# Opening a kernel from a list of steps, with fourteen of its transposes turned ahead of the first product

## The chip, the cores and the metric

The kernel runs on one core of a Trainium2 chip. The metric is device time in microseconds of one execution, the median over several runs. The engines that matter are TensorE (matmuls and transposes; the profile's PE, with PEld for the loading of its stationary operand), VectorE (DVE), ScalarE (ACT), GpSimd (POOL) and SyncE (SP), which here only issues DMAs. Each engine works through its own instructions in order; between engines, instructions wait on semaphores.

## The reference, cut to what matters

One layer of a diffusion backbone: 128 context tokens and 1024 latent tokens with 1024 features are normalized and modulated, projected by one weight matrix into two groups of attention heads (queries, keys, values, gates), run through a global and a windowed attention, gated, projected back and added to the residual stream.

```python
shift, scale, gate = modulation(c, w_mod[l], b_mod[l])          # silu(c) @ w_mod + b_mod
h = rmsnorm(xs, norm_gain[l]) * (1.0 + scale) + shift
q_a, k_a, v_a, g_a, q_b, k_b, v_b, g_b = project(h, w_in[l], ...)
...
xs = xs + gate * merge_out(o_a, g_a, o_b, g_b, w_out[l])
```

The change concerns only how `h` is made, and the first product with it: the gates `g_a` of group A.

## The kernel before, in words

Tokens are cut into nine tiles of 128 (`x` tile 0 is the context, 1 to 8 are latent), features into eight blocks of 128, numbered j or k. The products need `h` with features on the partitions, so each 128x128 block of `x` is transposed on TensorE against an identity (`turned`, line 606) into a PSUM bank, and from there `transposed` (line 610) makes `h`: ScalarE applies scale and shift of block j (line 617, into `hf`), VectorE casts the result to the high part of `h` (line 622), and GpSimd subtracts that from `hf` to get the low part (line 623). Every product is made of three matmuls: high weight by high `h`, low by high (lines 467, 468) and high by low (line 463). Tokens stand in the order 1, 2, ..., 8, 0 and are cut into three groups of 512, 256 and 384 columns (`THIRDS`): tiles 1 to 4, tiles 5 and 6, tiles 7, 8 and 0.

Ahead of a transpose an x tile is normalized: `norm` (line 589) squares it on ScalarE with a running sum (line 594; for tile 4 the second half on VectorE, line 597), GpSimd turns the sum into a reciprocal root (lines 601 and 603), and `scaled` multiplies the tile by it in place (line 587 on VectorE, 585 on ScalarE). Scale and shift of block j come from `modulate_rows(j)` (line 545: 16 small matmuls of the modulation weights `wm[j]`, 1 MB each, and a copy `mrows` out of PSUM, line 556) and `modulate(j)` (line 558: two transposes of `mrows`, then `columns`, lines 568 to 572, which fill `a_mod` and `b_col`). The weights of the gates arrive as eight chunks `rawga` of 256 KB (three buffers); `high` casts a chunk on ScalarE (line 435), `low` makes the rest on VectorE (line 440) and issues the load of a further chunk (line 443).

The opening is the part from the start to the end of the gate product of the first two token groups. Its order is written out by hand as a loop over j = 0 to 9 (line 661) with tables beside it (`LOADS`, `WARM`, `TURNED`, `BEHIND`, `PAIRED`). The first passes do this: tiles 1 and 2 are normalized and scaled on VectorE, 16 matmuls on the identity keep TensorE busy (`warm`, line 628), `modulate_rows(0)`, the two transposes of block 0 of tiles 1 and 2, `modulate(0)`, norms of tiles 3 and 4, then `h` of block 0 and its product in halves (`first_half`, line 642, its matmuls on line 648). From j = 2 each pass makes `modulate_rows(j)`, then the product of block j - 1 for four output blocks (`first_gates`, line 639) into four PSUM banks `big`, and between its parts `modulate`, the weights' split and `transposed(j, 1, 4, 0)`, that is four transposes for tiles 1 to 4. Later passes add the transposes of tiles 5 to 8 and 0, and the product of the second group (`next_gates`, line 651) into two banks `small`. At the end the product of the third group follows (`gates`, line 505). The transposes take two banks in turn, D and E (`bank_tr`); the eight banks are thus all named, but the four of `big` hold nothing until the first gate product.

All loads go through SP's queue in program order. A buffer is loaded again once its last reader is done: `wm` has three buffers, so wm3 follows `modulate_rows(0)`.

Of the kernel before, what the change touches and what calls it, by code (L numbers as in the profile page):

```python
# [11 lines left out]
F32 = mybir.dt.float32  # L12
# [8 lines left out]
P = 128  # L21
# [29 lines left out]
X_FROM = 2  # L51
SECOND_FROM = 5
LOADS = (1, 2, "m", 3, 4, "w", "m", "w", "m", 5, 6)
WARM = (16, 1, 5)
FULL = 1
MROWS_ACT = (7,)
SOON = 8
PAIRED = (4, 6)

TURNED = ((), (), (), (0,), (1, 2), (3,), (4, 5), (6, 7), (), ())  # L60
BEHIND = ((), (), (), (), (0,), (1, 2), (3,), (4, 5), (6,), (7,))
WIDE = 5
# [237 lines left out]
def hybrid_step(ctx, tc, x_prompt, x_sample, cache_k_a, cache_v_a, cache_k_b, cache_v_b,  # L300
# [48 lines left out]
    def bank_tr(name):  # L349
        turn["tr"] += 1  # L350
        return bank("DE"[turn["tr"] % 2], name)
# [53 lines left out]
    class Weights:  # L405
# [32 lines left out]
        def low(self, k, h, l):  # L438
            eng = nc.gpsimd if self.tag in POOL_LO and k % 2 else nc.vector
            eng.tensor_tensor(l, self.raw[k], h, op=ALU.subtract)  # L440
            self.hi.append(h)
            self.lo.append(l)
            self.load()
# [73 lines left out]
    with tc.tile_pool(name="st", bufs=2, side="right") as st:  # L517
# [9 lines left out]

        def load_wm(j):
# [45 lines left out]
        xn = {}  # L574

        def load_x(t):
            xn[t] = st.tile([P, D], F32, name=f"xn{t}", bufs=1)
            nc.sync.dma_start(xn[t], x_tile[t])
# [27 lines left out]
        def turned(px, j, t0, n):  # L606
            for i in range(n):
                nc.tensor.transpose(px[:, P * i : P * i + P], xn[t0 + i][:, P * j : P * j + P], ident)

        def transposed(j, t0, n, cond, px=None):  # L610
            if px is None:
                px = bank_tr(f"px{j}_{t0}")
                turned(px, j, t0, n)
# [3 lines left out]
            nc.scalar.activation(hf[:, :w], px[:, :w], AF.Identity,  # L617
                                 scale=a_mod[:, j, cond : cond + 1], bias=b_col[:, j, cond : cond + 1])
# [5 lines left out]

        for step in LOADS:
            load_x(step) if step in FIRST else W_GA.load() if step == "w" else load_wm(len(wm))

        def warm(n):

            for _ in range(n):  # L630
                nc.tensor.matmul(small[0], ident_b, ident_b.unsqueeze(1).to_broadcast([P, 4, P]), start=True, stop=True)

        rest = [7, 8, 0]
        second = [(j, 7, 2, 0) for j in range(WIDE)] + [(j, 0, 1, 1) for j in range(KT)]

# [19 lines left out]
        def more():  # L655
            ready = [x for x in second if x[0] <= j]
            if ready and j >= SECOND_FROM:
                second.remove(ready[0])
                transposed(*ready[0])

        for j in range(KT + 2):
            if j == 0:
                for t in (1, 2):
                    norm(t)
                    scaled(t)
                warm(WARM[0])
                modulate_rows(0)
                turned(small[1], 0, 1, 2)
                warm(WARM[1])
                modulate(0)  # L670
                warm(WARM[2])
                norm(3)
                norm(4, True)
                scaled(3, slice(0, 2 * P))
                transposed(0, 1, 2, 0, small[1])
                hi = W_GA.high()
                scaled(4, slice(0, 2 * P), nc.scalar)
                W_GA.low(*hi)
                first_half(0, 0)
                transposed(0, 3, 2, 0)  # L680
                modulate_rows(1)
                first_half(0, 1, 2)
                load_wm(3)
                continue
            if j == 1:
                modulate(1)
                W_GA.split()
                transposed(1, 1, 4, 0)
                first_half(1, 0, 1, 2)
                scaled(3, slice(2 * P, D))  # L690
                scaled(4, slice(2 * P, D), nc.scalar)
                load_wm(4)
                norm(5)
                continue
            big_on, behind = j <= KT, BEHIND[j]
            if SOON <= j < KT:
                W_GA.split()
            if j < KT:
                if j in PAIRED:
                    modulate_rows(j, j + 1)  # L700
                elif j - 1 not in PAIRED:
                    modulate_rows(j)
                if j + 3 < KT:
                    load_wm(j + 3)
                if X_FROM <= j < X_FROM + 3:
                    load_x(rest[j - X_FROM])
            if big_on:
                first_gates(0, j - 1, 0)
                first_gates(1, j - 1, 0)
            if j == 3:  # L710
                scaled(6)
            if 2 <= j < SOON:
                if j - 1 not in PAIRED:
                    modulate(*((j, j + 1) if j in PAIRED else (j,)))
                W_GA.split()
                transposed(j, 1, 4, 0)
            if big_on:
                first_gates(0, j - 1, 1)
                first_gates(1, j - 1, 1)
            if j == 2:  # L720
                norm(6)
                scaled(5)
            if big_on:
                first_gates(2, j - 1)
            if SOON <= j < KT:
                modulate(j)
                transposed(j, 1, 4, 0)
            if big_on:
                first_gates(3, j - 1)
            if X_FROM + 1 < j <= X_FROM + 4:  # L730
                scaled(rest[j - X_FROM - 2])
            for n in TURNED[j]:
                transposed(n, 5, 2 if n < WIDE else 4, 0)
            if X_FROM < j <= X_FROM + 3:
                norm(rest[j - X_FROM - 1])
            for ch in range(4):
                for n in behind:
                    next_gates(ch, n)
                if ch % 2 or j >= KT:
                    more()  # L740
            if j == KT:
                sg_tile.append(lambda n: st.tile([P, 512], F32, tag="sg", name=n, bufs=3))
                for ch in range(FULL):
                    put_gates(big[ch], 0, ch, slice(0, 512), nc.sync)
            if KT - 2 <= j < KT:
                raw = st.tile([P, KT, 2, P], F32, tag="wm", name=f"raw_qa{j}", bufs=3).rearrange(
                    "p (k a) s n -> p k (a s n)", a=2)
                k0 = 4 * (j - KT + 2)
                c0, n = W_QA.cols[0]
                nc.sync.dma_start(  # L750
                    raw, w_in[P * k0 : P * k0 + 512, c0 : c0 + n].rearrange("(k p) n -> p k n", p=P))
                W_QA.raw += [raw[:, k] for k in range(4)]
        assert not second


# [884 lines left out]
```

## Time and profile before

| what | us |
|---|---|
| median of 3 runs (668.84 to 669.23) | 669.11 |
| the profiled execution | 669.37 |
| its span, first to last instruction | 667.5 |
| TensorE busy in it | 655.5 |
| first gate product starts at | 14.78 |
| `modulate_rows(3)` starts at | 25.49 |
| product of the third group starts at | 66.9 |

Times within the profile count from the start of the span. A row of the timeline gives start, length, engine, line, operation, the output and input tiles, how often, and in brackets how long the engine stood idle before it and what released it. TensorE's matmuls overlap, and their ends are modelled, so the length of a single one is longer than the step from one to the next; the chain of waits gives the steps. Rows of groups give busy time, mean length in ns and idle time before them.

### The profile page before, as it was taken

How to read it: one execution, taken by the hardware profiler on the slowest of the kernel's cores; microseconds unless marked ns; L12 is line 12 of the kernel's file. 1: busy time of each engine (PE TensorE's matmuls, PEld its weight loads, DVE VectorE, ACT ScalarE, POOL GpSimd, SP SyncE). 2: the span in 40 equal slices, each digit the busy share in tenths (PEclk: the TensorE clock that was granted, in tenths of full speed). 3: DMA queues.
4: the chain of work that ended last, by engine and by line, in shares of the span. 5: the costliest groups of instructions: out<-in, count | busy, mean ns of one | idle time of the engine just before them, and what ended most of it. 6: DMA issues, size and time to landing. Idle time of an engine off the chain costs nothing.

```text
span 667.5 us, 10648 instructions
## 1 busy us (share of the span) xinstructions
PE 655.5 (98%) x3757; PEld 517.5 (78%) x3757; DVE 438.6 (66%) x924; ACT 281.3 (42%) x586; POOL 332.3 (50%) x324
## 2 busy tenths in 40 slices
PE   6999999999999999999999999999999999999997
PEld 2789988887788788997777777777777777777766
DVE  3566147786684766446768878688787786875533
ACT  4555411242142453435554355444454355434531
POOL 2457013332321232357885575657665675557712
PEclk9999999999999999999999999999999999999999
DMA  8980365437645211744142302223132212332233
GB/s 323 413 304 6 131 231 151 91 77 224 185 108 146 91 48 37 224 127 148 56 132 100 99 31 97 89 72 96 41 119 88 72 53 83 124 92 78 76 103 111
DMA packets 55837, 81.41 MB, mean 122 GB/s; under 512 B 7388, under 2 KB 26932, under 8 KB 54760
## 3 DMA queue, kind: packets, MB, share of 16 engines
q1 hardware_dynamic: 47752, 69.06, 30.9%
q10 hardware_dynamic: 8032, 11.68, 6.9%
q8 instruction: 30, 0.49, 0.3%
q14 instruction: 23, 0.19, 0.1%
HBM read 61.42 MB, written 19.29 MB: 121 GB/s over the span
## 4 chain that ended last, share of the span: by engine, by line
PE 92%; DVE 2%; ACT 2%; DMA 2%; issue 1%; ACTq 1%; SPq 0%; POOL 0%; DVEq 0%
PE pv L1432 15%; PE po L1507 15%; PE st L1390 7%; PE st L1391 7%; PE pmx L1130 5%; PE pq L454 4%; PE pq L455 4%; PE pq L453 4%; PE pg L468 3%; PE pg L463 3%; PE pg L467 3%; PE pk L454 2%; PE pk L455 2%; PE pk L453 2%; PE pmx L1133 2%; DMA xn<-in_x_sample_dram 1%
## 5 line engine op out<-in xcount | busy, mean ns | idle before, releaser
L1415 POOL TENSOR_TENSOR acc<-acc,pe 128x512 f32<-128x512 f32 x112 | 150.0, 1339 | 6.8 <-ACT pe L1402 0.6
L1402 ACT ACTIVATE pe<-st 128x512 f32<-128x512 f32 x208 | 120.4, 594 | 65.0 <-PE st L1391 52.3
L1143 DVE TENSOR_REDUCE mx<-pmx 128x1 f32<-128x384 f32 x192 | 104.4, 553 | 34.9 <-PE pmx L1130 32.1
L1432 PE MATMUL pv<-pe,v_all 128*64 128x256 f32 x832 | 96.8, 381 | 0.0
L1432 PEld LDWEIGHTS pv<-pe,v_all 128*64 128x64 f32 x832 | 58.3, 137 | 33.0 <-PE st L1391 4.2
L1507 PE MATMUL po<-wo,ogh 128*128 128x512 f32 (+1 forms) x224 | 79.5, 387 | 0.0
L372 POOL TENSOR_TENSOR rs_q<-ms_q,mhalf 128x8 f32<-128x8 f32 x18 | 34.8, 1931 | 80.1 <-DVE ms_q L370 80.1
L1130 PE MATMUL pmx<-kha,qt 128*128 128x384 f32 x192 | 64.1, 347 | 0.0
L1390 PE MATMUL st<-qt,kha 128*128 128x512 f32 x144 | 57.4, 398 | 0.5 <-ACT pe L1402 0.5
L1391 PE MATMUL st<-qb,kla 65*128 65x512 f32 x144 | 57.1, 396 | 0.0
L1148 DVE CUSTOM_DVE_ANT_0 pmx<-pmx,mask,nsink 128x512 f32<-128x512 f32 (+1 forms) x64 | 44.2, 722 | 11.4 <-PE pmx L1133 11.4
L1507 PEld LDWEIGHTS po<-wo,ogh 128*128 128x128 f32 x224 | 41.6, 189 | 9.5 <-ACT ogh L1469 0.6
L1464 POOL TENSOR_TENSOR spare<-spare,sgl 128x256 f32<-128x256 f32 x27 | 19.5, 735 | 50.0 <-DVE spare L1460 47.5
L1130 PEld LDWEIGHTS pmx<-kha,qt 128*128 128x128 f32 x192 | 35.3, 189 | 11.4 <-issue 5.0
L1507 PE MATMUL po<-wo,ogl 128*128 128x512 f32 (+1 forms) x112 | 43.2, 386 | 0.0
L1415 DVE TENSOR_TENSOR acc<-acc,pe 128x512 f32<-128x512 f32 x28 | 34.3, 1226 | 5.2 <-ACT pe L1402 3.9
L623 POOL TENSOR_TENSOR h<-hf,h 128x256 fp32r<-128x256 f32 (+2 forms) x33 | 28.0, 864 | 19.2 <-DVE h L622 19.2
L861 ACT ACTIVATE sqq<-pq 128x512 f32<-128x512 f32 x18 | 10.8, 599 | 53.6 <-DMA qd<-qo0q 15.7
L1390 PEld LDWEIGHTS st<-qt,kha 128*128 128x128 f32 x144 | 27.2, 189 | 5.7 <-ACT pe L1402 1.2
L467 PE MATMUL pg<-h,whigb 128*128 128x512 f32 (+2 forms) x88 | 30.0, 341 | 0.0
L1391 PEld LDWEIGHTS st<-qb,kla 65*128 65x128 f32 x144 | 27.0, 188 | 3.5
L468 PE MATMUL pg<-h,wlogb 128*128 128x512 f32 (+2 forms) x88 | 29.7, 337 | 0.0
(231 smaller groups left out, 1495.4 us busy)
## 6 DMA issues: line engine op xcount, KB each, us to landing
qt<-qd SPq DMA_DIRECT2D x36, 256.0 KB
wm<-in_w_mod_ss_dram SPq DMA_DIRECT2D x8, 1024.0 KB
qd<-qo0q ACTq DMA_DIRECT2D x36, 128.0 KB
qd<-qo1q ACTq DMA_DIRECT2D x36, 128.0 KB
qb<-qd SPq DMA_DIRECT2D x36, 128.0 KB
sgl<-gd SPq DMA_DIRECT2D x36, 128.0 KB
out_dram<-yt SPq DMA_DIRECT2D x17, 256.0 KB
xn<-in_x_sample_dram SPq DMA_DIRECT2D x8, 512.0 KB
```

The costliest lines, as they stand in the source:

```text
L453: nc.tensor.matmul(out, h_at(0, i, k, tok), w.hi[k], start=(k == 0), stop=False)
L467: nc.tensor.matmul(out, w.hi[k][:, cs], h_at(0, i, k, to), start=(k == 0 and first), stop=False)
L468: nc.tensor.matmul(out, w.lo[k][:, cs], h_at(0, i, k, to), start=False, stop=False)
L1130: nc.tensor.matmul(pm[:, 0:384], lhs, kha[:, g, 3 * b : 3 * b + 3, :], start=True, stop=True)
L1143: nc.vector.tensor_reduce(mx[:, h, b : b + 1], pm[:, 0:384], axis=AX.X, op=ALU.max)
L1148: nc.vector.tensor_tensor_reduce(s, s, mask[:, m0 : m0 + P * (p1_ - p0)], -1.0, nsink[:, 4 * g + h : 4 * g + h + 1], op0=ALU.add, op1=ALU.min,
L1390: nc.tensor.matmul(s, kh, qtile[i], start=True, stop=False)
L1391: nc.tensor.matmul(s, kl, qbtile[i], start=False, stop=True)
L1402: nc.scalar.activation(pe, v["s"], AF.Exp)
L1415: (nc.vector if (m, b) in ADD_DVE else nc.gpsimd).tensor_tensor(acc[i], first, pe, op=ALU.add)
L1432: nc.tensor.matmul(pv[HD * s : HD * s + HD, o : o + 256].rearrange("p (c n) -> p c n", c=2), lhs, r[:, :, s, :], start=start, stop=stop)
L1507: nc.tensor.matmul(po[c], x, wo_parts[KT * n + k][lo][:, q], start=(k == KS[0] and p == 0), stop=(k == KS[-1] and p == 2))
```

## The change

The loop and its tables go. A tuple `OPENING` names every step of the opening in order, and a short loop runs it. Beside the list there are these new things:

- `x14`: tiles 1 to 4 of x are slices of one SBUF tile instead of four tiles.
- `early(b, j0, n, t0)`: transposes n blocks, from j0 on, of tiles t0 and t0 + 1 into bank `big[b]`; `kept(b, j0, n, t0, on_act)` copies them from the bank back to where these blocks stood in `x14`, on ScalarE or VectorE. The list does so for blocks 1 to 7 of tiles 1 and 2: 14 transposes and four copies. `own` remembers them; `turned` skips them, and `transposed` reads that half from `x14` in an activation of its own.
- `load_wm_part`: wm0 is loaded in two halves.
- The loads of gate weights are steps of the list and no longer issued by `low`.

The order changes in places. Tile 2 is scaled on ScalarE. Ten matmuls on the identity stand ahead of `modulate_rows(0)` and three behind `modulate(0)`, instead of 16, 1 and 5. Chunk 1 of the gate weights is loaded ahead of wm1, x8 ahead of wm6. `half(0, 1)` stands ahead of `modulate_rows(1)`; for j = 1 `high` and `low` stand behind `h`, for the other blocks ahead of the transposes. The norms, scalings and products of the second group, and the last transposes of tile 0, are spread differently between the products.

```diff
-        for j in range(KT + 2):
-            if j == 0:
-                for t in (1, 2):
-                    norm(t)
-                    scaled(t)
-                warm(WARM[0])
-                modulate_rows(0)
-                turned(small[1], 0, 1, 2)
-                warm(WARM[1])
-                modulate(0)
...
+OPENING = (('x', 1), ('x', 2), ('wm2', 0, 0), ('wm2', 0, 1), ('x', 3), ('x', 4), ('w',), ('w',), ('wm',), ('wm',),
+           ('x', 5), ('x', 6), ('norm', 1), ('scaled', 1), ('norm', 2), ('scaled', 2, 0, 8, True), ('warm', 10),
+           ('rows', 0), ('turn', 0, 1, 2, True), ('early', 1, 3, 2, 1), ('early', 0, 1, 2, 1),
+           ('early', 2, 5, 2, 1), ('early', 3, 7, 1, 1), ('kept', 0, 1, 2, 1, False), ('kept', 1, 3, 2, 1, True),
+           ('kept', 2, 5, 2, 1, False), ('kept', 3, 7, 1, 1, True), ('mod', 0), ('warm', 3), ('norm', 3),
+           ('norm', 4, True), ('scaled', 3, 0, 2), ('h', 0, 1, 2, 0), ('high',), ('scaled', 4, 0, 2, True),
+           ('low',), ('half', 0, 0), ('w',), ('turn', 0, 3, 2), ('h', 0, 3, 2, 0), ('half', 0, 1), ('rows', 1),
+           ('half', 0, 2), ('wm',), ('mod', 1), ('w',), ('turn', 1, 1, 4), ('h', 1, 1, 4, 0), ('high',), ('low',),
+           ('half', 1, 0), ('scaled', 4, 2, 8, True), ('half', 1, 1), ('half', 1, 2), ('wm',), ('norm', 5),
+           ('scaled', 3, 2, 8), ('rows', 2), ('wm',), ('x', 7), ('big', 0, 1, 0), ('big', 1, 1, 0), ('mod', 2),
+           ('high',), ('low',), ('w',), ('big', 0, 1, 1), ('big', 1, 1, 1), ('turn', 2, 1, 4), ('norm', 6),
+           ('scaled', 5), ('h', 2, 1, 4, 0), ('big', 2, 1), ('big', 3, 1), ('rows', 3), ('x', 8), ('big', 0, 2, 0),
+           ('wm',), ('w',), ('big', 1, 2, 0), ('scaled', 6, 0, 8, True), ('mod', 3), ('high',), ('low',),
...
+           ('small', 3, 2), ('scaled', 8), ('turn', 3, 5, 2), ('h', 3, 5, 2, 0), ('norm', 0),
+           ('small', 0, 1), ('small', 0, 2), ('small', 1, 1), ('small', 1, 2), ('turn', 0, 7, 2), ('h', 0, 7, 2, 0),
...
         def turned(px, j, t0, n):
             for i in range(n):
+                if (j, t0 + i - (t0 + i + 1) % 2) in own:
+                    continue
                 nc.tensor.transpose(px[:, P * i : P * i + P], xn[t0 + i][:, P * j : P * j + P], ident)
...
-            nc.scalar.activation(hf[:, :w], px[:, :w], AF.Identity,
-                                 scale=a_mod[:, j, cond : cond + 1], bias=b_col[:, j, cond : cond + 1])
+            for i in range(0, n, 2 if (j, t0) in own or (j, t0 + 2) in own else n):
+                at = slice(P * i, w if n < 2 or (j, t0) not in own and (j, t0 + 2) not in own else P * i + 2 * P)
+                if (j, t0 + i) in own:
+                    out = hf[:, at].rearrange("p (t c) -> p t c", c=P)
+                    x = x14[:, t0 + i - 1 : t0 + i + 1, P * j : P * j + P]
+                else:
+                    out, x = hf[:, at], px[:, at]
+                nc.scalar.activation(out, x, AF.Identity,
+                                     scale=a_mod[:, j, cond : cond + 1], bias=b_col[:, j, cond : cond + 1])
...
+        def early(b, j0, n, t0):
+            at[b] = big[b] if b < 4 else small[0] if b == 4 else bank_tr(f"pe{b}")
+            for i in range(n):
+                for k in range(2):
+                    nc.tensor.transpose(at[b][:, P * (2 * i + k) : P * (2 * i + k) + P],
+                                        xn[t0 + k][:, P * (j0 + i) : P * (j0 + i) + P], ident)
+
+        def kept(b, j0, n, t0, on_act=False):
+            (nc.scalar.copy if on_act else nc.vector.tensor_copy)(
+                x14[:, t0 - 1 : t0 + 1, P * j0 : P * (j0 + n)].rearrange("p t (j c) -> p j t c", c=P),
+                at[b][:, 0 : 2 * P * n].rearrange("p (j t c) -> p j t c", t=2, c=P))
+            own.update((j0 + i, t0) for i in range(n))
```

In the list `rows` is `modulate_rows`, `mod` is `modulate`, `turn` the transposes of `turned`, `h` is `transposed`, `half` is `first_half`, `big` is `first_gates`, `small` is `next_gates`, and `x`, `w`, `wm` and `wm2` are loads.

More of the change, by code (lines that the diff above doesn't have):

```diff
@@ L55 @@
 FULL = 1
 MROWS_ACT = (7,)
[L57 to L62, printed above, removed]
 POOL_LO = ("gb",)
@@ L753, in hybrid_step, with turn_x, queries_raw @@
-        assert not second
+        px = {}
+        def turn_x(j, t0, n, first=False):
+            px[j, t0] = small[1] if first else bank_tr(f"px{j}_{t0}")
+            turned(px[j, t0], j, t0, n)
+        def queries_raw(half):
+            raw = st.tile([P, KT, 2, P], F32, tag="wm", name=f"raw_qa{half}", bufs=3).rearrange(
+                "p (k a) s n -> p k (a s n)", a=2)
+            k0 = 4 * half
+            c0, n = W_QA.cols[0]
+            nc.sync.dma_start(
+                raw, w_in[P * k0 : P * k0 + 512, c0 : c0 + n].rearrange("(k p) n -> p k n", p=P))
+            W_QA.raw += [raw[:, k] for k in range(4)]
@@ L756, in hybrid_step @@
+        for name, *args in OPENING:
+            act[name](*args)
         for ch in range(FULL, 4):
```

146 lines of the change are left out of this document (46 added, 100 removed).

## The prediction

> **What bounds the kernel now.** I read the page first, for its totals and for the chain of work that ended last.
>
> ```profile
> span 667.5 us, 10648 instructions
> PE 655.5 (98%) x3757; PEld 517.5 (78%) x3757; DVE 438.6 (66%) x924; ACT 281.3 (42%) x586; POOL 332.3 (50%) x324
> PE 92%; DVE 2%; ACT 2%; DMA 2%; issue 1%; ACTq 1%; SPq 0%; POOL 0%; DVEq 0%
> ```
>
> TensorE is busy for 98% of the span, and the chain lies on it. A change pays only if it takes TensorE work away or fills one of its gaps, so I asked next where the gaps are: the windows view, cut into four stretches (PE busy is the first figure after the length; the last three are granted clock, DMA share and GB/s).
>
> ```profile
> 0.00:15.00 15.00, 9.43 (x44) 3.77 (x45) 4.84 (x16) 6.63 (x12) 4.07 (x13) 1.00 0.80 310
> 15.00:30.00 15.00, 14.40 (x116) 10.73 (x116) 8.42 (x23) 8.17 (x13) 6.40 (x9) 1.00 1.02 414
> 30.00:70.00 40.00, 39.84 (x303) 34.33 (x302) 24.04 (x52) 21.65 (x39) 25.69 (x35) 1.00 0.48 181
> 70.00:667.50 597.50, 591.79 (x3299) 468.67 (x3297) 401.27 (x835) 244.90 (x522) 296.15 (x268) 1.00 0.35 106
> ```
>
> PE is idle 5.57 us before 15 us (and much of the rest there is warming matmuls), 0.60 from 15 to 30, 0.16 from 30 to 70. From 15 to 30 us the DMA engines are full at 414 GB/s. So the opening has free TensorE time only in its first 15 us. The timeline of that stretch shows what the first gate product (L648) waits for:
>
> ```profile
> 2.97 6.08 PE L631 MATMUL pg_s<-ident_b 128*128 128x512 bf16 x16 [2.97 <-DVE ident_b L521]
> 10.31 1.07 PE L551 MATMUL pm<-wm,sil 128*32 128x256 f32 x16 [1.27 <-DMA wm<-in_w_mod_ss_dram]
> 11.55 1.06 ACT L594 ACTIVATE sq<-xn 128x1024 bf16<-128x1024 f32 x1 [3.57 <-DMA xn<-in_x_sample_dram]
> 12.86 0.63 ACT L594 ACTIVATE sq<-xn 128x512 bf16<-128x512 f32 x1 [0.15 <-DMA xn<-in_x_sample_dram]
> 13.06 0.96 POOL L603 TENSOR_TENSOR rsx<-msx,mhalf 128x1 f32<-128x1 f32 x1
> 13.49 0.55 ACT L617 ACTIVATE hf<-pg_s,b_col,a_mod 128x256 f32<-128x256 f32 x1
> 14.06 0.37 DVE L587 TENSOR_SCALAR xn<-xn,rsx 128x256 f32<-128x256 f32 x1 [0.43 <-POOL rsx L603]
> 14.36 0.27 DVE L622 CAST h<-hf 128x256 fp32r<-128x256 f32 x1
> 14.78 0.72 PE L648 MATMUL pg_f<-h,whiga 128*128 128x256 f32 x4 [1.34 <-DVE h L622]
> ```
>
> It is a chain off TensorE: the third x tile lands at 11.55, ACT squares it, GpSimd makes its rsqrt, VectorE scales it (14.06) and only then casts h (14.36), because VectorE runs in program order; the product follows at 14.78. Everything that ACT or VectorE does between 11.5 and 14.6 pushes it back.
>
> Two places behind it matter: TensorE waits again ahead of `modulate_rows(3)`, and once at the end of the opening.
>
> ```profile
> 22.32 0.62 ACT L435 CAST whiga<-rawga 128x512 fp32r<-128x512 f32 x1 [0.44 <-DMA rawga<-in_w_in_dram]
> 25.49 1.07 PE L551 MATMUL pm<-wm,sil 128*32 128x256 f32 x16 [0.50 <-DVE xn L587]
> 26.03 0.62 ACT L435 CAST whiga<-rawga 128x512 fp32r<-128x512 f32 x1 [0.74 <-DMA rawga<-in_w_in_dram]
> 66.39 0.14 PEld L608 LDWEIGHTS px<-ident,xn 128*128 128x128 f32 x1 [0.36 <-ACT hf L617]
> ```
>
> The page names VectorE's scaling for 25.49, but `modulate_rows(3)` reads nothing of it. It reads wm3, which stands in SP's queue between the weight chunks w2 (landed at 22.32) and w3 (26.03); w3's 0.26 MB at 414 GB/s take 0.63, so wm3 landed near 25.4. The change leaves the bytes ahead of wm3 as they are and the DMA engines are full, so **TensorE can't pass this point before about 25.4, however early it comes**.
>
> **The change part by part.** Prices first, from the chain of waits (start, length, what), the groups by form, one source line, and the timeline.
>
> ```profile
> 18.25 0.22 PE pm L562 x2
> 18.91 1.43 PE pg_f L648 x12
> 20.34 1.00 PE pm L551 x16
> 21.34 0.43 PE pg_f L467
> 21.77 0.24 PE pg_f L468
> 33.85 0.44 PE px L608 x4
> ...
> L556 DVE COPY mrows<-pm 128x256 f32<-128x256 f32 x6 | 2.4, 421 | 3.3 <-PE pm L551 3.3
> L617 ACT ACTIVATE hf<-px,b_col,a_mod 128x512 f32<-128x512 f32 x10 | 7.7, 777 | 10.6 <-DVE b_col L572 4.8 <-DVE m L568 3.6 <-PE px L608 1.3
> L617 ACT ACTIVATE hf<-px,b_col,a_mod 128x256 f32<-128x256 f32 x10 | 5.5, 564 | 6.6 <-PE px L608 6.0 <-POOL h L623 0.6
> ...
> L892 ACT CAST qo0q<-ptq x18: 577/586/587, 106.0 to 208.6; 128x512 fp32r<-128x512 f32 x18
> ...
> 15.63 0.14 PEld L608 LDWEIGHTS px<-ident,xn 128*128 128x128 f32 x1 [0.26 <-ACT xn L585]
> 18.51 0.17 DVE L568 TENSOR_REDUCE m<-pm 128x4 f32<-128x16 f32 x1 [0.93 <-PE pm L562]
> 18.92 0.22 DVE L572 TENSOR_SCALAR b_col<-m,colt 128x2 f32<-128x2 f32 x1
> 19.05 0.68 DVE L440 TENSOR_TENSOR wloga<-rawga,whiga 128x512 fp32r<-128x512 f32 x1
> 19.91 0.93 ACT L585 ACTIVATE xn<-xn,rsx 128x768 f32<-128x768 f32 x1
> ```
>
> A transpose costs 0.11 in a stream (0.44 for four).
>
> *Removed.* Blocks 1 to 7 of tiles 1 and 2 leave the later turns: 14 transposes, 1.54 us of TensorE. Four of them (j = 1, 2) stand ahead of `modulate_rows(3)`, ten (j = 3 to 7) behind it: 1.1 us where TensorE has no gap.
>
> *Added at the start.* `rows(0)` still waits for wm0. Its two halves let 8 of the 16 matmuls run early, so it ends 0.5 sooner, near 10.8. Behind it stand two turns and the 14 early transposes, 16 x 0.11 = 1.8, so the last ends near 12.6, with its result some 0.2 later. `kept(3)` (ACT, 256 columns out of PSUM) then runs 12.8 to 13.2. No row has this copy; its bounds are half of 0.586 and the 0.564 of L617, and I take 0.42, what VectorE needs for that size (L556). `kept(1)` (0.6, L892) fits ahead of it. On VectorE `kept(0)` and `kept(2)` (512 columns out of PSUM) lie between 0.42 and twice that; I take 0.69, and they end near 13.6, ahead of what comes next.
>
> What pays is ACT: the square of tile 3, at 11.55 before, stands behind `kept(3)` and starts at 13.2. The whole chain to L648 hangs on it and moves by 1.65: **first product near 16.4** (16.3 to 16.6 by the bounds of `kept(3)`). Scaling tile 2 on ACT (1024 columns, by L585 about 1.15 instead of VectorE's 0.75) ends near 10.1 and hides behind the wait for wm0; without that cover it would cost the 0.4.
>
> *From the first product to `modulate_rows(3)`.* TensorE's work there: 24 half products 2.86, two rows 2.0, twelve 512-column products 12 x 0.23 + 0.2 (the first behind rows takes 0.43), two `mod` 0.44, three turns of two 0.66: 8.96, so 25.4 if nothing stalled, just when wm3 lands. I count four stalls. (1) `turn(0,3,2)` waits for ACT's scaling of tile 4, as before (15.63): 0.3. (2) `half(0,1)` now stands ahead of `rows(1)`, so only `half(0,2)` covers the mrows copy ahead of `mod(1)`: 0.42 and two hand-overs against 0.47, 0.2 to 0.3. (3) For j = 1 `high` and `low` now stand behind `h`, and the own half is a second activation: from the end of `rows(1)`, mrows 0.42, mod 0.22, columns 0.63 (18.51 to 19.14), two activations 1.1, high 0.62, low 0.68 and six hand-overs of 0.1 make 4.3, against TensorE's 0.67 + 0.44 + 1.43 + 1.0 + 0.43 = 4.0: 0.3. (4) The mrows copy of j = 2 stands on VectorE behind that `low` and the scaling of tile 3 (0.61): 0.3. With 1.2 of stalls `modulate_rows(3)` starts near 26.6, **1.15 later than before**. The bounds are 25.5 (no stall) and 27.2 (each stall half as long again).
>
> *Behind it.* 1.1 us of transposes go, and the 0.36 at the end may go, since the last turns now stand between products. New: `h(2,...)` stands on ACT behind the square of tile 6 (1.06), so the first product of j = 2 waits about 0.4 for its cast; `turn(0,7,2)` stands right behind the scaling of tile 8 and may wait 0.3. Each of j = 1 to 7 costs ACT 2 x 0.56 in place of 0.78, 0.34 more; with ACT busy 21.65 of the 40 us that hides, and only the cast comes 0.3 later. Together -1.1 - 0.36 + 0.7 = -0.75.
>
> *Moved at no cost.* On SP's queue w1 now precedes wm1, x8 precedes wm6, and w3 waits for a later `low(0)` with wm4, wm5 and x7 behind it. By 15 us 4.65 MB have landed (15 x 310 GB/s), while the loads through wm3 are 8.2 MB, so the engines have some 8 us of work queued; w3, wm4 and the rest come in well within it. If the queue ran dry each us would go straight into the wait for wm5. POOL moves nothing but its own later inputs.
>
> **Sum**: +1.15 - 0.75 = +0.4 us. The profiled execution took 669.37 (span 667.5 and 1.87 around it), so 669.8; the median of the runs shown, 669.11, lies 0.26 lower, hence **669.5**. Behind 70 us nothing is edited, and TensorE is busy 591.8 of 597.5 there, so a shift is carried to the end. A measurement of this kernel can tell about 0.2%, 1.34 us, from no change.
>
> **The rivals.**
>
> *The start is paid back (faster).* If the stalls stay away, the later first product eats only time that TensorE spent waiting for wm3, and the ten transposes and the 0.36 remain: -1.46, 667.65. For it: 25.4 without stalls is right at wm3's landing. Against: the mrows, `high` and `low` orders above, and the first product must be no later than 16.4.
>
> *TensorE at half pace (slower).* The loads of the warming matmuls show a slow start:
>
> ```profile
> 3.37 0.15 PEld L631 LDWEIGHTS <-ident_b 128*128 128x128 bf16 x1 [0.27 <-issue]
> 7.64 0.15 PEld L631 LDWEIGHTS <-ident_b 128*128 128x128 bf16 x1 [0.28 <-issue]
> 8.02 0.53 PEld L631 LDWEIGHTS <-ident_b 128*128 128x128 bf16 x3 [0.23 <-issue]
> ```
>
> They come 0.43 apart from 3.37 to 7.64 and 0.2 apart from 8.02, with the granted clock at 1.00 throughout: TensorE doubled its pace after 4.7 to 5 us of unbroken work. Ten warming matmuls end at 2.97 + 10 x 0.43 = 7.25, before that point, and then it idles for the halves of wm0. If the pace never doubles there, the second half of `rows(0)` and 16 transposes take twice as long: 0.4 + 1.5, all of it ahead of the first product, so +0.4 + 1.9 = +2.3, 671.4. It decides at whether 4.3 us are enough; speaking against it, most of the stretch before 8 us is still filled.
>
> The Trainium skill ("TensorE: Matmul & The Clock Gate", Part 1) has a rule for this: full rate comes after one busy window of about 3.4 us, and the windows run free of the kernel's start. The trace agrees (a window that ended near 7.8 and held only work). By that rule ten matmuls hold a whole window only if it begins in their first 0.9 us, sixteen in every case; the same page (Part 4) says that transposes don't count as busy the same way, which no row here shows.
>
> *The change doesn't do what it says.* Tiles 1 to 4 now share one SBUF tile. If an access to one slice were held for the whole tile, the square of tile 1 would wait for tile 4 (12.86 instead of 5.14), some 8 us: 677.
>
> ```profile
> 36.34 0.36 PE L467 MATMUL pg_s<-h,whiga 128*128 128x256 f32 x1
> ...
> 37.06 1.08 DVE L622 CAST h<-hf 128x256 fp32r<-128x256 f32 x2 [0.42 <-ACT hf L617]
> ```
>
> Against it: blocks 0 and 1 of the second token group share one h tile, the cast of block 1 is issued ahead of the product of block 0, and the product ran (36.34) before that cast (37.06). Only what overlaps is waited for.
>
> **How the numbers follow.** Forecast 0.57 (its own range 668.4 to 670.1: the sum with `modulate_rows(3)` at 25.5 to 27.2), paid back 0.19, half pace 0.20, shared tile 0.04. Predicted 669.5; from 667.5 to 671.4 I leave out the shared tile and the outer parts of the two other rivals, 0.2 together. Faster 0.19, same 0.57, slower 0.24.
>
> **What would show it.** First product near 16.4 with ACT's third square near 13.2; `modulate_rows(3)` near 26.6 and behind PE work, not a load; two transposes in place of four in each later turn of tiles 1 to 4; no wait of 0.36 at the end. Wrong if the square of tile 3 starts before 12.8, if transposes ahead of 13 us are 0.2 apart (half pace), or if TensorE reaches wm3 before it has landed (paid back).

## The result and the profile after

| kernel | median us | lowest to highest | runs | ratio, 95% interval |
|---|---|---|---|---|
| before | 669.12 | 668.84 to 670.11 | 6 | |
| after | 673.08 | 671.96 to 673.29 | 6 | 1.0054 [1.0043, 1.0064] |

The change costs 3.96 us, 0.6%. The prediction, 669.5 with a range up to 671.4, was too low: it had forecast no change clear of 0.2%. One execution of all the runs below was slow (815.48 us, granted clock 0.75, of the kernel before with x tile 6 moved) and stays out of its ratio.

The profiled execution took 673.05, with a span of 671.3. The windows view, cut as for the kernel before (length, PE, PEld, DVE, ACT, POOL, granted clock, DMA share, GB/s):

```profile
0.00:15.00 15.00, 9.97 (x47) 5.56 (x47) 3.72 (x12) 6.29 (x10) 2.18 (x9) 0.89 0.83 308
15.00:30.00 15.00, 11.63 (x81) 8.01 (x80) 8.37 (x22) 9.51 (x20) 7.74 (x11) 0.89 1.01 406
30.00:70.00 40.00, 39.66 (x305) 33.04 (x305) 25.30 (x55) 23.24 (x43) 25.09 (x32) 1.00 0.46 169
70.00:671.30 601.30, 595.55 (x3321) 472.70 (x3319) 401.93 (x838) 248.01 (x528) 298.03 (x272) 1.00 0.35 106
```

Two things are new, both before 30 us. TensorE is idle for 3.37 us from 15 to 30 (0.60 before), and the granted clock is 0.89 where it was 1.00. Behind 30 us nothing of size has changed.

The chain of waits of the same execution gives the places (start, length, what; in this kernel L587 is `modulate_rows`, L647 the turns, L713 the early transposes, L685 the half products):

```profile
10.12 0.64 PE pm L587 x8
...
11.21 3.00 PE pg_f L713 x14
...
14.50 1.16 ACT sq L631 x2
...
17.64 1.10 PE pg_f L685 x4
...
20.02 1.56 PE pm L587 x16
...
30.06 1.00 PE pm L587 x16
```

The 14 early transposes took 3.00 us, 0.21 each instead of 0.11. The first product began at 17.64 (before: 14.78), `modulate_rows(3)` at 30.06 in this view and 29.99 in the timeline (before: 25.49). So 4.50 us are lost up to there. The product of the third group began at 66.90 by the timeline of the kernel before, and at 70.49 by that of the changed kernel (L467 there and L497 here are the first matmul of a product):

```profile
66.90 0.34 PE L467 MATMUL pg<-h,whiga 128*128 128x384 f32 x1
```

```profile
70.49 0.40 PE L497 MATMUL pg<-h,whiga 128*128 128x384 f32 x1
```

That is 3.59 later: behind `modulate_rows(3)` 0.91 us came back. The two profiled executions differ by 3.68.

Windows of 1 us over the same stretch show the clock (the column before the DMA share):

```profile
9.00:10.00 1.00, 0.59 (x8) 0.11 (x8) 0.00 (x0) 1.00 (x1) 0.00 (x0) 1.00 0.99 406
10.00:11.00 1.00, 0.88 (x10) 0.47 (x11) 0.18 (x1) 0.06 (x1) 0.00 (x0) 0.95 1.04 426
11.00:12.00 1.00, 1.00 (x7) 1.00 (x6) 0.25 (x1) 0.00 (x0) 0.00 (x0) 0.50 1.01 408
...
14.00:15.00 1.00, 1.00 (x6) 0.55 (x5) 0.89 (x4) 0.77 (x2) 0.00 (x0) 0.84 1.06 442
15.00:16.00 1.00, 0.18 (x1) 0.00 (x0) 0.42 (x3) 0.97 (x3) 0.19 (x1) 1.00 0.99 410
...
17.00:18.00 1.00, 0.36 (x2) 0.39 (x3) 1.00 (x3) 0.44 (x2) 0.92 (x3) 0.87 0.94 389
18.00:19.00 1.00, 1.00 (x7) 1.00 (x7) 0.09 (x1) 0.44 (x1) 0.69 (x1) 0.50 0.99 401
...
21.00:22.00 1.00, 1.00 (x16) 0.49 (x6) 0.34 (x1) 0.00 (x0) 0.00 (x0) 0.93 1.08 428
```

The clock is halved twice. Read the partial windows as a mix of 1.00 and 0.50: 0.95 puts the first halving at 10.9, 0.84 its end at 14.3, 0.87 the second halving at 17.7, 0.93 its end near 21.1. Each lasts 3.4 us, and so does the full clock between them. The 3.4 us ahead of each halving held little TensorE work: 10.9 back to 7.5 about 1.4 us (the 0.59, and 0.8 of the next window), 17.7 back to 14.3 about 0.9. The first halved stretch held nothing but transposes (the two turns, the 14 early ones and those of `modulate(0)`), and full clock came back at its end all the same. The second took the first half products and `rows(1)`, 1.56 instead of 1.00.

The timeline shows TensorE's gaps in those thin stretches and the second loss, at the `mrows` of j = 2 (L592 copies `mrows`, L624 scales x tile 3, L469 is the split by `low`, L666 is GpSimd's subtraction for `h`, L717 is `kept`; in brackets the idle time before):

```profile
8.96 0.64 PE L587 MATMUL pm<-wm,sil 128*32 128x256 f32 x8 [1.54 <-DMA wm<-in_w_mod_ss_dram]
...
14.23 0.37 ACT L717 COPY x<-pg_f 128x256 f32<-128x256 f32 x1 [1.50 <-PE pg_f L713]
...
17.64 1.10 PE L685 MATMUL pg_f<-h,whiga 128*128 128x256 f32 x4 [2.45 <-DVE h L665]
...
24.88 1.84 POOL L666 TENSOR_TENSOR h<-hf,h 128x512 fp32r<-128x512 f32 x1 [3.97 <-DVE h L665]
24.88 0.69 DVE L469 TENSOR_TENSOR wloga<-rawga,whiga 128x512 fp32r<-128x512 f32 x1
...
25.49 1.64 DVE L624 TENSOR_SCALAR x<-x,rsx 128x768 f32<-128x768 f32 x1
...
27.53 0.44 PE L598 MATMUL pm<-ident,mrows 128*128 128x128 f32 x2 [0.92 <-DVE mrows L592]
```

VectorE's scaling of tile 3 took 1.64 us where the kernel before needs 0.61 for the same shape (20.39 in its timeline, below), and it ends (27.13) only after GpSimd's subtraction (26.72). In the kernel before a subtraction ran beside it too, but began behind it (20.55) and took 1.59; here the subtraction had begun 0.61 us earlier (24.88) than the scaling (25.49). The `mrows` copy stands behind it, and TensorE waits 0.92 us.

```profile
20.39 0.61 DVE L587 TENSOR_SCALAR xn<-xn,rsx 128x768 f32<-128x768 f32 x1
```

My theory after this reading: the clock is the larger part, the scaling behind the subtraction about 0.9, and the rest is the order of the list. The rivals: the early turning itself (its copies on ScalarE ahead of the third square), and wm3, which would hide whatever is repaired ahead of it.

### The profile page after: what moved, and what is told of

It is laid out like the page before. It is cut to its first block, busy times and chain, and to the rows that moved or that the text cites. A ratio compares the mean times of both kernels' runs of the same rounds, so it can differ in the third digit from the quotient of the medians.

```text
span 671.3 us, 10635 instructions
## 1 busy us (share of the span) xinstructions
PE 656.8 (98%) x3748; PEld 519.3 (77%) x3748; DVE 439.3 (65%) x923; ACT 287.0 (43%) x598; POOL 333.0 (50%) x324
## 4 chain that ended last, share of the span: by engine, by line
PE 91%; DVE 3%; ACT 2%; DMA 1%; issue 1%; ACTq 1%; POOL 1%; SPq 0%; DVEq 0%
PE pv L1415 15%; PE po L1490 15%; PE st L1373 7%; PE st L1374 7%; PE pmx L1113 5%; PE pq L484 4%; PE pq L485 4%; PE pq L483 4%; PE pg L497 3%; PE pg L498 3%; PE pg L493 3%; PE pk L484 2%; PE pk L485 2%; PE pk L483 2%; PE pmx L1116 2%; PE ptq L872 1%
## 5 line engine op out<-in xcount | busy, mean ns | idle before, releaser
L666 POOL TENSOR_TENSOR h<-hf,h 128x256 fp32r<-128x256 f32 (+2 forms) x33 | 27.5, 847 | 20.3 <-DVE h L665 20.3
L844 ACT ACTIVATE sqq<-pq 128x512 f32<-128x512 f32 x18 | 10.8, 598 | 53.4 <-DMA qd<-qo0q 17.3
L497 PE MATMUL pg<-h,whigb 128*128 128x512 f32 (+2 forms) x88 | 30.0, 341 | 0.0
```

The source lines that it names most:

```text
L497: nc.tensor.matmul(out, w.hi[k][:, cs], h_at(0, i, k, to), start=(k == 0 and first), stop=False)
```

## The experiments

### More warming matmuls, at both places and at one

The first run restores the warming counts of the kernel before or more, at both places; the two others at one.

```diff
-('warm', 10), ('rows', 0), ... ('mod', 0), ('warm', 3),
+('warm', 16), ('rows', 0), ... ('mod', 0), ('warm', 13),    both
+('warm', 16), ('rows', 0), ... ('mod', 0), ('warm', 3),     first
+('warm', 10), ('rows', 0), ... ('mod', 0), ('warm', 13),    last
```

> The changed kernel with 16 warming matmuls ahead of modulate_rows(0) instead of 10, and 13 behind modulate(0) instead of 3, so that TensorE has work from 7.4 to 9.0 and from about 13.5 to 16.3. Theory (half pace): the 4 us were lost because TensorE, after idling from 7.4 to 10.7 and from 15.2 to 17.6, ran two stretches of 3.4 us at a granted clock of 0.5 (10.9 to 14.3 and 17.7 to 21.1). Both go: clock 1.00 throughout, the 14 early transposes take 1.6 instead of 3.0, first product near 16.4, modulate_rows(3) at 26.6 to 27.3, time 669.5 to 670.2. Rival (long chain): the copies and the longer way to the first product cost the 4 us, and the low clock fell into waiting; then the time stays above 672.

> The changed kernel with 16 warming matmuls ahead of modulate_rows(0), the 3 behind modulate(0) kept. Half pace: the first slow stretch goes (transposes 1.6 instead of 3.0, first product near 16.4), the second, from about 17.7, stays because TensorE idles from 13.5 to 16.4; time about 671.3. Long chain: about 673.

> The changed kernel with its 10 warming matmuls ahead of modulate_rows(0), and 13 instead of 3 behind modulate(0). Half pace: the first slow stretch stays (first product at 17.6), the second goes; modulate_rows(3) near 28.4, time about 671.5. Long chain: about 673.

| kernel | median us | ratio to before, 95% interval |
|---|---|---|
| both | 670.57 | 1.0022 [1.0013, 1.0031] |
| first place alone | 671.92 | 1.0041 [1.0026, 1.0056] |
| second place alone | 672.14 | 1.0046 [1.0031, 1.0061] |

Nothing but matmuls on the identity was added, and the kernel is 2.51 us faster. One place alone gives 1.16 or 0.94; these are medians of four executions each (670.39 to 672.88 and 671.47 to 672.73), so the two sizes are rough. All three times lie 0.4 to 0.6 above what I had expected. The chain of the first:

```profile
11.34 1.54 PE pg_f L713 x14
...
16.31 0.71 PE pg_f L685 x4
...
22.95 1.57 DVE x L624
...
27.44 1.00 PE pm L587 x16
```

The early transposes take 1.54, as I had priced them, and the first product begins at 16.31, 0.1 from the forecast and 1.33 earlier than in the changed kernel; by `modulate_rows(3)` (27.44 for 30.06) the lead has grown to 2.62, and the further 1.29 is the second halving's part. The scaling still takes 1.57, and `modulate_rows(3)` is still 1.9 us later than in the kernel before: the clock wasn't all.

The chain of the run with warming at the first place alone, and one of its windows of 5 us, show the first halving gone and the second left:

```profile
11.39 0.64 PE pm L587 x8
...
12.40 1.54 PE pg_f L713 x14
...
17.37 0.96 PE pg_f L685 x4
```

```profile
15.00:20.00 5.00, 2.63 (x18) 2.15 (x22) 2.35 (x8) 3.14 (x8) 3.02 (x6) 0.76 1.00 412
```

Its first product begins at 17.37 and not near 16.4 as I had expected, because the second half of wm0 landed 1.3 us later in this execution (11.39) than in the changed kernel's (10.12). A start that is read from one trace is no surer than that.

The run with warming at the second place alone has a trap in it. These rows are of its chain and of its windows of 5 us:

```profile
10.51 1.08 PE pm L587 x8
12.21 3.00 PE pg_f L713 x14
```

```profile
10.00:15.00 5.00, 4.93 (x31) 3.68 (x26) 1.31 (x3) 0.79 (x2) 0.00 (x0) 1.00 1.05 427
```

Eight matmuls of `rows(0)` take 1.08 instead of 0.64 and the transposes 3.00, both half pace, yet the clock column says 1.00. In these traces the column stands at 1.00 until a first halving is recorded, also while the first warming matmuls run at half pace; the spacing of the matmuls is the safer sign. By the timeline all 16 matmuls of `rows(0)` took 2.23 here: in this execution the pace had not doubled by then, which is the condition of the prediction's rival. It was full behind 15.2, after 3.4 us filled with transposes.

### The warming counts alone, in the kernel before

```diff
-WARM = (16, 1, 5)
+WARM = (10, 0, 3)
```

> The kernel before with the warming counts of the changed kernel: 10, 0 and 3 matmuls instead of 16, 1 and 5, nothing else. Half pace, by counts alone: TensorE idles from 7.3 to 10.3, so its work from 10.9 on runs at half pace for 3.4 us or longer, and perhaps a second stretch of products behind 14.8; time 670 to 672. Rival (the counts matter only with the longer start): the 0.6 us of slack ahead of modulate_rows(3) hides it, 669.0 to 669.5.

Measured: 670.92 (669.38 to 673.14), 1.0028 [1.0017, 1.0039], beside 669.07 for the kernel before. With its own order and not one early transpose the kernel loses 1.85 us to the counts of the change. Its ten times spread over 3.8 us. That fits a clock decided in windows that don't begin with the kernel: the same few matmuls sometimes do and sometimes don't hold it. No trace shows the slower of the ten; the profiled execution is the second fastest (669.55). Its windows view:

```profile
10.00:15.00 5.00, 3.86 (x23) 1.91 (x14) 2.79 (x9) 3.34 (x7) 2.92 (x5) 0.55 1.02 416
15.00:20.00 5.00, 5.00 (x42) 3.50 (x42) 1.77 (x6) 1.43 (x3) 0.91 (x2) 0.77 1.02 412
```

Read as before, 0.55 and 0.77 make 6.8 us at half pace, two stretches of 3.4 in a row. It is still only 0.2 us over the profiled execution of the kernel before. Its x tile 3 landed earlier, at 10.67 (11.55 there), and its first product began at 14.13 (14.78), which likely hides part of the loss.

### The list without the early turning

```diff
-('early', 1, 3, 2, 1), ... ('early', 3, 7, 1, 1), ('kept', 0, 1, 2, 1, False), ... ('kept', 3, 7, 1, 1, True),
-('warm', 10), ... ('warm', 3),
+('warm', 16), ... ('warm', 9),
```

The 14 transposes are then done in their later turns again; nothing else of the list changes.

> The changed kernel's list without the 14 early transposes and their four copies (the later turns make them, as before), with 16 warming matmuls ahead of modulate_rows(0) and 9 behind modulate(0) so that the clock holds. Half pace: what is left is the new order alone; first product near 14.8, modulate_rows(3) at 25.5 to 26.2, time 669.0 to 669.8, so that the turning ahead is worth within 0.7 us either way beside warm_both. Long chain: the copies were the loss, so this is as fast as the kernel before and 3 us faster than warm_both.

Measured: 670.09 (669.67 to 670.77), 1.0014 [1.0005, 1.0024]. That is 0.3 above my range. So 1.0 us over the kernel before (669.08 beside these runs) comes from what else the change does, its order above all. With the turning it is 670.57, 0.48 more, but the two ranges overlap, and in the profiles the product of the third group starts at 67.87 in both. The chain of this run has the slow scaling again, with no early transpose in the kernel:

```profile
22.20 1.57 DVE x L622
```

### The scaling of tile 3 ahead of the subtraction, and the split ahead of `h`

Both go on from the run with warming at both places. The first moves one step, the second moves another two as well:

```diff
-('half', 1, 2), ('wm',), ('norm', 5), ('scaled', 3, 2, 8), ('rows', 2),
+('half', 1, 2), ('wm',), ('norm', 5), ('rows', 2),
 ...
-('turn', 0, 3, 2), ('h', 0, 3, 2, 0), ('half', 0, 1),
+('turn', 0, 3, 2), ('h', 0, 3, 2, 0), ('scaled', 3, 2, 8), ('half', 0, 1),
```

```diff
-('turn', 1, 1, 4), ('h', 1, 1, 4, 0), ('high',), ('low',),
+('turn', 1, 1, 4), ('high',), ('low',), ('h', 1, 1, 4, 0),
```

> warm_both with one step moved: the scaling of blocks 2 to 7 of tile 3 stands behind h of block 0 of tiles 3 and 4, where VectorE is idle, instead of behind the low part of chunk 1, where it took 1.6 instead of 0.6 us while GpSimd ran a subtraction, with the mrows copy of block 2 behind it. Theory (VectorE held up by GpSimd): this 1.6 us on VectorE is what TensorE waits for ahead of modulate(2); it falls to 0.6, the wait of 0.9 goes, modulate_rows(3) comes at 26.5 instead of 27.4 and the time falls by 0.8 to 0.9, to about 669.7. Rival (the chain is held elsewhere): the wait passes to the cast of h or to the load of wm3, and the time falls by less than 0.3.

> The run with the scaling moved, with the split of the weights of j = 1 (high on ScalarE, low on VectorE) ahead of the scale and cast of j = 1 again, as in the kernel before. My step (3) priced this order at 0.3 us: then 669.65 falls to about 669.3. Rival (that wait lies beside the landing of weights 1 or another wait and costs nothing): no change, 669.6.

| kernel | median us | lowest to highest | ratio to before, 95% interval |
|---|---|---|---|
| scaling moved | 669.65 | 669.16 to 670.33 | 1.0010 [1.0000, 1.0019] |
| and split first | 669.18 | 668.99 to 669.53 | 1.0000 [0.9991, 1.0009] |

The timeline of the first:

```profile
18.74 0.61 DVE L624 TENSOR_SCALAR x<-x,rsx 128x768 f32<-128x768 f32 x1
...
18.91 1.04 POOL L666 TENSOR_TENSOR h<-hf,h 128x256 fp32r<-128x256 f32 x1 [1.15 <-DVE h L665]
...
26.82 0.42 PE L587 MATMUL pm<-wm,sil 128*32 128x256 f32 x4
```

and of the second:

```profile
16.75 0.72 PE L685 MATMUL pg_f<-h,whiga 128*128 128x256 f32 x4 [0.42 <-DVE h L665]
...
22.70 1.29 POOL L666 TENSOR_TENSOR h<-hf,h 128x512 fp32r<-128x512 f32 x1 [2.71 <-DVE h L665]
...
26.41 1.07 PE L587 MATMUL pm<-wm,sil 128*32 128x256 f32 x16
```

Where the scaling begins ahead of a subtraction (18.74, and 18.91 on GpSimd) it takes 0.61, the subtraction is the longer one (1.04, where one of its size takes 0.73 in the kernel before, at 31.70), and 0.92 us are gone. The order of the split is worth another 0.47, though the two intervals overlap. With three repairs (2.51 + 0.92 + 0.47 = 3.90 of the 3.96) the kernel stands where it stood before, its fourteen transposes still turned early. So, as far as differences of medians tell, the loss lies in these three places. It also shows that the turning as such brings nothing here: between the first product (1.97 later than before) and the end of the opening the saved transposes are used up.

### Turning in the idle time, with the order of before

If the start weren't late, the ten transposes behind `modulate_rows(3)` should show as a gain. These two kernels turn tile 1 ahead of `rows(0)` and tile 2 between its two halves, so that the copies end ahead of the third square. The first keeps the order of before otherwise, the second takes the order of the change from `modulate_rows(3)` on.

```diff
-('warm', 10), ('rows', 0), ('turn', 0, 1, 2, True), ('early', 1, 3, 2, 1), ... ('kept', 0, 1, 2, 1, False), ...
+('warm', 13), ('early', 1, 3, 2, 1, 0), ... ('rows0', 0), ('early', 1, 3, 2, 1, 1), ...
+('kept', 0, 1, 2, 1, False), ('kept', 1, 3, 2, 1, True), ('rows0', 1), ('kept', 2, 5, 2, 1, False), ...
-                for k in range(2):
+                for k in (range(2) if only is None else (only,)):
...
-                for k in range(KT):
+                for k in range(KT) if half is None else range(4 * half, 4 * half + 4):
```

> The order of the kernel before, with blocks 1 to 7 of tiles 1 and 2 turned ahead of modulate_rows(0) instead of behind it: those of tile 1 as soon as it is scaled, the first half of modulate_rows(0), those of tile 2, the second half. Tile 2 is scaled on VectorE as before; 13 warming matmuls ahead, 9 behind modulate(0). Theory (the place of the turning costs, not the turning): the copies end near 11.5, before the square of tile 3 could start, so the first product comes near 14.9, modulate_rows(3) at 25.4 to 25.6 where wm3 lands, and the ten transposes behind it are won: 667.7 to 668.4. Rival (the second activations and the copies cost as much as the transposes): 668.8 to 669.5.

> early_first up to modulate_rows(3), the changed kernel's order from there on. From modulate_rows(3) to the product of the third group the profiles give 41.4 for the kernel before and 40.6 for warm_both; early_first should win the ten transposes there too. If the changed order of this part is worth something of its own (no wait at the end), this is 0.1 to 0.4 faster than early_first; if not, equal within 0.1.

Measured: 669.51 (669.30 to 671.60), 1.0010 [1.0001, 1.0020], and 669.57 (668.99 to 670.13), 1.0005 [0.9996, 1.0014]. Neither gains, where I had expected 667.7 to 668.4 of the first. The first kernel's profiled execution is the highest of its ten times (671.60), so the timeline is that of the second (its line numbers are three higher):

```profile
15.01 0.71 PE L688 MATMUL pg_f<-h,whiga 128*128 128x256 f32 x4 [0.48 <-DVE h L668]
...
26.18 1.07 PE L590 MATMUL pm<-wm,sil 128*32 128x256 f32 x16 [1.47 <-DMA wm<-in_w_mod_ss_dram]
```

The first product is nearly on time, and TensorE then reaches `modulate_rows(3)` early and waits 1.47 us for wm3 to land, where the kernel before waited 0.50. The saved transposes have become idle time: 0.69 late at `modulate_rows(3)`, this kernel is level with the kernel before at the product of the third group (66.91 for 66.90). wm3 landed at 26.18 here, some 0.8 later than the 25.4 of the prediction with the same loads ahead of it; no run shows why.

### One load moved out of the way

If wm3's landing is the bound, x tile 6, 512 KB issued ahead of it, should be issued behind it. This was done to the kernel before and to the second kernel of the last part:

```diff
-LOADS = (1, 2, "m", 3, 4, "w", "m", "w", "m", 5, 6)
+LOADS = (1, 2, "m", 3, 4, "w", "m", "w", "m", 5)
...
                 load_wm(3)
+                load_x(6)
```

> The kernel before with one load moved: x tile 6 (512 KB) is issued behind modulation weights 3 instead of ahead of them. The DMA engines are busy without a break there (1.0 of their time at 380 to 440 GB/s from 20 to 27 us), so weights 3 should land 512 KB / 0.41 MB per us = 1.3 us earlier. Theory (their landing near 25.4 us is the point that TensorE cannot pass before): the 0.49 us that TensorE stands idle before modulate_rows(3) at 25.49 goes, and it starts near 25.0; time 668.5 to 668.7. Rival (TensorE is as late by its own work, the landing is beside the point): modulate_rows(3) stays near 25.5, time 669.1.

> The hybrid with the same load moved behind weights 3. In the hybrid's trace modulate_rows(3) began at 26.18 with 1.47 us idle before it, ended by the landing of weights 3. Theory (the 14 transposes less do show, but as waiting for that landing): with weights 3 landing 1.3 us earlier modulate_rows(3) begins near 24.9 and the time falls by 1.0 to 1.3 us, to 668.3 to 668.6, under the kernel before (669.1). Rival (x tile 6 or another tile is late next, or the hybrid's lateness has another cause): 669.3 to 669.6.

Measured: 668.77 (0.9995 [0.9986, 1.0004]) and 669.49 (1.0005 [0.9996, 1.0013]), beside 669.13. In the kernel before, `modulate_rows(3)` moved from 25.49 to 24.85 with no wait before it, and the median fell by 0.36:

```profile
24.85 1.07 PE L551 MATMUL pm<-wm,sil 128*32 128x256 f32 x16
```

This median is the lowest of all, but its interval holds 1. In the other kernel the landing moved and the time didn't, as the rival had it. Its timeline:

```profile
24.88 1.07 PE L590 MATMUL pm<-wm,sil 128*32 128x256 f32 x16 [0.41 <-DVE h L668]
...
26.11 1.06 ACT L634 ACTIVATE sq<-xn 128x1024 bf16<-128x1024 f32 x1 [1.73 <-DMA xn<-in_x_sample_dram]
...
28.21 1.15 ACT L625 ACTIVATE xn<-xn,rsx 128x1024 f32<-128x1024 f32 x1 [0.95 <-POOL rsx L643]
...
30.88 0.42 PE L590 MATMUL pm<-wm,sil 128*32 128x256 f32 x4 [1.13 <-ACT hf L663]
```

1.3 us were won at wm3 and lost at the next landing: tile 6 arrives (26.11), is squared and scaled on ScalarE, and the scale of j = 3 behind it holds TensorE up for 1.13 us. One more run moved that scaling to VectorE:

```diff
-('scaled', 6, 0, 8, True),
+('scaled', 6),
```

> The run before (hybrid, x tile 6 behind weights 3) with the scaling of tile 6 on VectorE, where the kernel before has it, instead of ScalarE. In the run before modulate_rows(3) did begin 1.3 us earlier (24.88), but modulate_rows(4, 5) stood idle for 1.13 us until 30.88: ScalarE's scale of j = 3 (29.77 to 31.2) waited behind the high halves (29.27), those behind the scaling of tile 6 (28.21, 1.15 us), and that for GpSimd's root at 28.1. Theory (the order of ScalarE around tile 6 gave the 1.1 us back): high halves near 27.3, scale of j = 3 done near 29.2, modulate_rows(4, 5) near 29.8, third group's products near 66.0, and the time falls by about 1.1 us to 668.4, under the kernel before (669.1) and about 0.4 under the kernel before with the load moved (668.8). Rival (the cast of j = 3 waits on VectorE behind the scaling and the low halves, and the wait moves to the products of j = 3): 669.1 to 669.4.

Measured: 669.35 (668.76 to 670.02), 1.0002 [0.9993, 1.0011]. My theory fell: the wait stayed, 1.11 us ahead of `modulate_rows(4, 5)`. VectorE in its order waited for GpSimd's root of tile 6 until 28.24, scaled, and only then took the columns of j = 3 (28.91), so that ScalarE had its scale and shift at 29.6 as late as before. Its timeline:

```profile
28.24 0.75 DVE L626 TENSOR_SCALAR xn<-xn,rsx 128x1024 f32<-128x1024 f32 x1 [1.77 <-POOL rsx L642]
28.91 0.17 DVE L606 TENSOR_REDUCE m<-pm 128x4 f32<-128x16 f32 x1
...
29.63 0.60 ACT L662 ACTIVATE hf<-x,b_col,a_mod 128x256 f32<-128x256 f32 x1 [1.83 <-DVE b_col L610]
```

Whether a further order around tile 6 would let the saved transposes show was not tried.

## Why the prediction was wrong, step by step

- **The bound: right place, not a fixed time.** wm3 as the point TensorE can't pass early is what the second of the turning runs waited for (1.47 us), and moving one load ahead of it moved it (25.49 to 24.85 in the kernel before). But it landed at 26.18 in that turning run, not near 25.4.
- **The start on ScalarE: right.** `kept(3)` took 0.37 (I took 0.42), and with the clock held the square of tile 3 began at 13.17 (13.2) and the first product at 16.31 (16.4). The transposes cost 0.11 each then.
- **The clock: the step that failed.** I left the half pace out of the sum and made it a rival with a chance of 0.20, because "most of the stretch before 8 us is still filled", and I made it hang on whether the pace ever doubles. It did double in the changed kernel's profiled execution: both halves of `rows(0)` ran at full pace (0.64 each). The clock was then taken back, twice, after 3.4 us with about 1.4 and 0.9 us of work in them, and the transposes came 0.21 apart, my own sign of half pace. I had priced 1.9 us, all ahead of the first product; the warming runs put 2.51 on it, in two about equal parts by the traces (1.33 and 1.29), the second behind the first product, where I had looked at no gap. The reduced second warming (3 for 5, with the first product later) I had not priced at all.
- **Stall (4): right place, wrong size.** I took 0.61 for the scaling of tile 3 and 0.3 for the wait. The scaling took 1.64 behind GpSimd's subtraction, the wait was 0.92, and moving the scaling gave 0.92.
- **Stall (3): right place, too small.** 0.3 forecast, 0.47 by undoing the order.
- **Stalls (1) and (2): about right.** In the run with all three repairs `modulate_rows(3)` follows the first product by 9.66 us (16.75 to 26.41), 0.74 over the work, whose terms add up to 8.92 and not to 8.96; I had put 0.5 to 0.6 on the two. No run takes them apart.
- **Behind `modulate_rows(3)`: about right.** -0.75 forecast, -0.91 measured (4.50 late there, 3.59 late at the third group's product). The wait of 0.36 at the end is gone; the other terms weren't taken apart.
- **Paid back: fell, for a reason I had named.** Even where the first product was on time, TensorE reached wm3 before it had landed, and repairing that ran into tile 6. **The shared tile: fell**; the square of tile 1 began at 5.31 (5.14 before), and that of tile 3 waited for `kept(3)` and no load of a neighbour.

Put together, my sum of +0.4 lacked 2.5 for the clock, 0.6 for stall (4) and 0.2 for stall (3), and had 0.16 too little behind `modulate_rows(3)`: +3.5, where the profiled executions differ by 3.68 and the medians by 3.96.

## What to carry to other kernels

Work that seems useless can hold the clock: before fewer warming matmuls or a longer wait go in, add up the matmul time in each stretch of some 3.4 us of the changed order, not only up to the first gap. Moving work into idle time pays only if what comes next on that engine isn't a landing: here the DMA engines were full from 15 to 30 us (share 1.01), and the saved transposes became a longer wait for wm3 or tile 6. The duration of an elementwise step holds only for the neighbour it had: moved on VectorE to where a subtraction on GpSimd had already begun, the scaling took nearly three times as long.

## What the runs showed of the hardware

- **The clock is taken back after a thin window, not only after an idle one.** Halved stretches of 3.4 us followed 3.4 us with 1.4 and 0.9 us of work; the longest single gaps ahead of them were 1.54 us (before 8.96) and 2.45 us (before 17.64). With warming at the first place alone, counted back in steps of 3.4 from the halving near 17.6, the stretch from 7.4 to 10.8 held 2.0 us of work with a gap of 1.43, and the next was not halved. Getting the clock back seems to take more: with the counts lowered in the kernel before, a halved stretch from 10.5 to 13.9 with 2.5 us of work was followed by another. Transposes count for this here, against what the prediction quotes on them: twice full clock came back after 3.4 us of nothing else (14.3 in the changed kernel, about 15.2 with warming at the second place). Where the limits lie no run tried. The Trainium skill ("TensorE: Matmul & The Clock Gate", Why this matters for your kernels) advises against idle gaps of more than about 3 us between bursts of matmuls. The trace differs: gaps of 1.54 and 2.45 us were enough here, and the measurement decides. Its window length (Part 1), about 3.4 us and not tied to the kernel's start, agrees with the stretches, and the spread of 3.8 us in the run that only lowered the warming counts fits it.
- **VectorE and GpSimd hold each other up in SBUF.** Which begins first decides. The same scaling took 1.64 where a subtraction had begun before it (24.88 and 25.49), and 0.61 where it began before the subtraction (20.39 and 20.55 in the kernel before, 18.74 and 18.91 with the scaling moved). Then the subtraction is held up: in the run with tile 6 moved, where VectorE's scaling (0.75) had begun first, GpSimd's subtraction took 1.72. Here is that timeline:

```profile
24.76 0.75 DVE L627 TENSOR_SCALAR xn<-xn,rsx 128x1024 f32<-128x1024 f32 x1
24.92 1.72 POOL L669 TENSOR_TENSOR h<-hf,h 128x512 fp32r<-128x512 f32 x1 [1.09 <-DVE h L668]
```

  In the run with the split first the same subtraction took 1.29 (22.70), with neither VectorE's scaling of tile 3 (done by 19.4) nor the split beside it. The Trainium skill ("Trainium Architecture — The Big Picture", What this means for kernel authors) says that VectorE and GpSimd share one pair of ports into SBUF under an exclusive lock. The two durations agree with that; no run here shows the lock itself.
